# A hybrid S5/SSD/MoE block on Trainium2: the decays' bound moves from VectorE to ScalarE, and the mixers' list scheduler gets other cost estimates

## Chip, cores and metric

One core of one Trainium2 chip. The metric is the device time of one execution in microseconds (us). The kernel before takes 1853.15 us, the median of three runs.

## What is computed

One layer of a diffusion-transformer block over 256 latent tokens and 256 context tokens of width 1024, all in float32: modulation from a condition, RMS norm, one input projection, two mixers (S5, a diagonal state space with 64 groups, and SSD, a chunked scan with 32 heads in 8 groups, both in two directions), gates and an output projection, and then a mixture of 32 experts with four chosen per token.

The change touches one piece of the SSD mixer, the decay matrix of a chunk. Cut to what matters:

```
def decay_matrix(a_cum):
    mask = jnp.tril(jnp.ones((q, q), dtype=bool))
    diff = a_cum[..., :, None] - a_cum[..., None, :]
    return jnp.where(mask, jnp.exp(jnp.where(mask, diff, 0.0)), 0.0)

lmat = decay_matrix(a_cum) * dt_t[..., None, :]
y_diag = jnp.einsum('bcgls,bcgrls,bcsgrp->bclgrp', cb, lmat, x)
```

With r for the cumulated decay of the row, c for that of the column and ln dt for the logarithm of the column's step, what the kernel needs is exp(min(r - c, 0) + ln dt). The bound at 0 keeps the half outside the mask from overflowing; the mask itself comes later, with the product by `cbm`.

## The kernel before

The program has four stages. **Front**: modulation, norm and the split of the normed input into a high and a low float32r part (`uh`, `ul`). **Mixers** (`mixers`, L465 and below): the input projection and both mixers, interleaved. **Projections**: the S5 gate `glu`, the branches `wa` and `wb`, the output `wo`, the router. **Experts** (`moe`): 32 experts, each with three 1024x1024 float32 matrices, streamed as 1 MB tiles `mw`. Their loads begin in the projections, where `paced` lets out the first twelve, and not earlier.

In the mixers every piece of work is a Python generator, a stream: `gemm` (the input projection, column by column), two of `conv`, `prep`, `ssd`, `decays`, `vgen`, `tables`, `states`, `outputs`, `sigmoids` and some small ones. A stream yields before each step and names the engine that the step starts on and what it needs. `Plan.run` is a list scheduler at build time: it keeps a clock for each engine and a time at which each tile is ready, takes the stream whose next step can start first, and among those on the same engine within `NEAR` = 260 ns the one that `PRIO` and `PACE` rank first. `Planned` advances the clocks by `cost`. So the numbers in `cost` never run on the chip; they set the order in which each engine's instructions stand, and an engine runs its instructions in that order. Since all of this goes through one recording helper, the trace shows nearly every instruction of the mixers at one line (L1442), and they are told apart by tile.

The streams that matter here:

- `gemm`: for each column a weight block `w` of 128x512 is loaded, cast to `h` on ScalarE (high part), subtracted into another `h` on VectorE or GpSimd (low part; line `lo = dve if ...` picks by the planned clocks), and used in 12 matmuls into one of two PSUM banks `mm`. It prepares `LOOK` = 2 blocks ahead. Column i waits until column i-2's bank is free.
- `conv`: takes the bank of an SSD column with one ScalarE instruction and four VectorE `SCALAR_TENSOR_TENSOR` (`cv<-mm,cw,cv`); the bank is free after the fourth. A `Silu` on ScalarE follows.
- `decays`: 16 steps n (8 groups, two directions). Each loads `rt` [128, 4, 256] (one buffer), fills `et` (two buffers), turns both into exponentials, and multiplies `rt` on GpSimd. Step n+1 starts when step n has been used by `ssd`.
- `ssd`: multiplies `et` by the masked `cbm` on VectorE and runs the matmuls `yps<-et,xtok` and `yps<-rt,bt`.
- `states`, `vgen`, `outputs`: S5, mostly VectorE (`V`, `Wt`, `rot`, `Y`, `l4a`).

Before the change a decay step has eight VectorE instructions of 128x128, `et = min(rt - acs, lnd)`, with `acs` holding c - ln dt, and then one `Exp` of 128x1024 over `et` and one over `rt`.

Of the kernel before, what the change touches and what calls it, by code (L numbers as in the profile page):

```python
# [13 lines left out]
AF = mybir.ActivationFunctionType  # L14
ALU = mybir.AluOpType
# [4 lines left out]
P = 128  # L20
# [26 lines left out]
def bcast(ap, axis, n):  # L47
    a = ap.unsqueeze(axis)
    shape = list(a.shape)
    shape[axis] = n  # L50
    return a.to_broadcast(shape)


def build(tc, I, out):
    nc = tc.nc
    dve, act, pe, pool, sp = nc.vector, nc.scalar, nc.tensor, nc.gpsimd, nc.sync
# [44 lines left out]
    def aux_ps(name="aux"):  # L101
        return ps.tile([P, 512], F32, tag="aux", name=name, bufs=2)
# [221 lines left out]
    for c in range(4):  # L324
# [12 lines left out]
        for k in (2 * c, 2 * c + 1):  # L337
            h_, l_ = uh[k // 4][:, k % 4], ul[k // 4][:, k % 4]
            for wh in range(2):
                o = slice(wh * 256, wh * 256 + 256)  # L340
                a, b = sc1[:, wh, k:k + 1], modc[:, wh, 0, k:k + 1]
# [4 lines left out]
    def mm3(out, a, b, first, last):  # L346

        pe.matmul(out, a[0], b[0], start=first, stop=False)
        pe.matmul(out, a[0], b[1], start=False, stop=False)  # L349
        pe.matmul(out, a[1], b[0], start=False, stop=last)  # L350
# [24 lines left out]
    def ux(n):  # L375
        return lambda k: (uh[k // 4][:, k % 4, 0:n], ul[k // 4][:, k % 4, 0:n])
# [8 lines left out]
    def ssd_dt():  # L385
        act.activation(arow, arow, AF.Exp)
        wdh = H.tile([P, KD, 64], F32R, tag="h", name="wdh")
        act.copy(wdh, wdt)
        wdl = H.tile([P, KD, 64], F32R, tag="h", name="wdl")
        dve.tensor_tensor(wdl, wdt, wdh.bitcast(F32), op=ALU.subtract)  # L390
        pd = aux_ps()
        for k in range(KD):
            mm3(pd[0:64], (wdh[:, k], wdl[:, k]), ux(512)(k), k == 0, k == KD - 1)
        dtr = F.tile([64, 512], F32, tag="Ut", name="dtr")
        act.copy(dtr, pd[0:64])
        pt = aux_ps()
        for t in range(4):
            pe.transpose(pt[:, t * 64:(t + 1) * 64], dtr[:, t * P:(t + 1) * P], ident[0:64, 0:64])
        n = [-1]
        dtt = F.tile([P, 4, 4, 64], F32, tag="et", name="dtt", bufs=2)  # L400
        dtt = [dtt[:, i] for i in range(4)] + [F.tile([P, 4, 64], F32, tag="xtok", name="dtq", bufs=BUFS["xtok"])]

        def tt():
            n[0] += 1
            return dtt[n[0]]

        x, e, s_, s2, q = tt(), tt(), tt(), tt(), tt()
        dve.tensor_tensor(x, pt[:, 0:256].rearrange("p (t c) -> p t c", t=4), bcast(dtb, 1, 4), op=ALU.add)
        act.activation(e, x, AF.Abs)
        act.activation(e, e, AF.Exp, scale=-1.0)  # L410

        dve.tensor_scalar(s_, e, 2.0, None, op0=ALU.add)
        dve.reciprocal(s_, s_)
        dve.tensor_mul(s_, s_, e)
        dve.tensor_mul(s2, s_, s_)
        dve.tensor_scalar(q, s2, 1.0 / 15, None, op0=ALU.mult)
        for c_ in (13, 11, 9, 7, 5, 3):
            dve.scalar_tensor_tensor(q, q, 1.0 / c_, s2, op0=ALU.add, op1=ALU.mult)
        dve.scalar_tensor_tensor(q, q, 1.0, s_, op0=ALU.add, op1=ALU.mult)
        dve.tensor_scalar(x, x, 0.0, None, op0=ALU.max)  # L420
        dt = F.tile([P, 4, 64], F32, tag="dg", name="dt")
        dve.scalar_tensor_tensor(dt, q, 2.0, x, op0=ALU.mult, op1=ALU.add)
        dtA = F.tile([P, 4, 64], F32, tag="Cn", name="dtA")
        dve.scalar_tensor_tensor(dtA, dt, -1.0, bcast(arow, 1, 4), op0=ALU.mult, op1=ALU.mult)

        pr = aux_ps()
        pc = aux_ps()
        for c_ in range(2):
            for d_, tr in ((0, triU), (1, triL)):
                cols = slice(32 * d_, 32 * d_ + 32)  # L430
                pe.matmul(pr[cols, c_ * P:(c_ + 1) * P], dtA[:, c_, cols], tr, start=True, stop=True)
                pe.matmul(pc[:, c_ * 64 + 32 * d_:c_ * 64 + 32 * d_ + 32], tr, dtA[:, c_, cols], start=True, stop=True)
        arows = F.tile([64, 256], F32, tag="us", name="arows")
        act.copy(arows, pr[0:64, 0:256])
        acd = dram.tile([64, 256], F32, name="acd")
        act.dma_start(acd, arows)

        lnd = F.tile([P, 2, 64], F32, name="lnd")
        act.activation(lnd, dt[:, 0:2], AF.Ln)
        acs = F.tile([P, 2, 64], F32, name="acs")  # L440
        dve.tensor_tensor(acs, pc[:, 0:128].rearrange("p (c h) -> p c h", c=2), lnd, op=ALU.subtract)

        pw = aux_ps()
        f_, b_ = slice(0, 32), slice(32, 64)
        terms = [
            [(triLs, 2, f_), (ones, 3, f_)], [(triLs, 3, f_)],
            [(triUs, 2, b_)], [(triUs, 3, b_), (ones, 2, b_)],
            [(triLs, 0, f_)], [(triUs, 1, b_)],
            [(ones, 0, f_)], [(ones, 1, b_)],
        ]  # L450
        for i, tl in enumerate(terms):
            for j, (m_, t_, cl) in enumerate(tl):
                pe.matmul(pw[:, 32 * i:32 * i + 32], m_, dtA[:, t_, cl], start=(j == 0), stop=(j == len(tl) - 1))
        wend = F.tile([P, 8, 32], F32, name="wend")
        act.activation(wend.rearrange("p a b -> p (a b)"), pw[:, 0:256], AF.Exp)
        for i, tk, cl in ((0, 2, f_), (1, 3, f_), (2, 2, b_), (3, 3, b_), (4, 0, f_), (5, 1, b_)):
            dve.tensor_mul(wend[:, i, :], wend[:, i, :], dt[:, tk, cl])
        dsm.update(lnd=lnd, acs=acs, wend=wend, acd=acd)
# [6 lines left out]
    def mixers():  # L465
        plan = Plan(nc)
        pe, dve, act, pool, sp = plan.pe, plan.dve, plan.act, plan.pool, plan.sp
        tile_, mark, slot = plan.tile, plan.mark, plan.slot
        EP, Bb, r8, root = s5["EP"], s5["Bb"], s5["r8"], s5["root"]
        lnd, wend, acs, acd = dsm["lnd"], dsm["wend"], dsm["acs"], dsm["acd"]  # L470
# [7 lines left out]
        n = 0  # L478
# [434 lines left out]
        def decays():  # L913

            for n in range(2 * NG):
                g, d_ = n // 2, n % 2
                plan.at("decay", n / (2 * NG))
                yield ("sp", slot("rt", 1)) + ((("used", n - 1),) if n else ())
                rt = tile_(F, [P, 4, 256], F32, "rt")
                sp.dma_start(rt, acd[32 * d_ + 4 * g:32 * d_ + 4 * g + 4, :].partition_broadcast(P))  # L920
                et = tile_(F, [P, 4, 256], F32, "et", 2)
                for h in range(4):
                    yield "dve", rt
                    for c_ in range(2):
                        hh = 32 * d_ + 4 * g + h
                        dve.tensor_scalar(et[:, h, c_ * P:(c_ + 1) * P], rt[:, h, c_ * P:(c_ + 1) * P],
                                          acs[:, c_, hh:hh + 1], lnd[:, c_, hh:hh + 1], op0=ALU.subtract, op1=ALU.min)
                yield "act", et, AF.Exp
                act.activation(et, et, AF.Exp)
                act.activation(rt, rt, AF.Exp)  # L930
                yield "pool", rt, ("cv", g, 3)
                pool.tensor_tensor(rt, rt, bcast(cv[g, 3][:, 0], 1, 4), op=ALU.mult)
                dec[n] = rt, et
                mark(("dec", n))
# [332 lines left out]
    for t in range(2):  # L1267
# [15 lines left out]
                                 op0=ALU.add, op1=ALU.mult))  # L1283
# [47 lines left out]
class Plan:  # L1331
# [28 lines left out]
    def mark(self, name):  # L1360
        self.ready[name] = self.last
# [46 lines left out]
def key(x):  # L1408
    return getattr(x, "tensor", x).name


class Planned:
# [33 lines left out]
    def cost(self, op, args, kw, out, ins, n):  # L1446
        plan, name = self.plan, self.name
        if name == "pe":
            wide = ins[0]
            m = math.prod(wide.shape[1:])  # L1450
            part = 0.25 if m <= 32 else 0.5 if m <= 64 else 1
            if op == "transpose":
                return 109 * wide.shape[0] / P
            return max(n, 16) * (4 if ins[1].dtype == F32 else 1) * 0.42 * part
        if name == "act":
            f = next((a for a in args if isinstance(a, AF)), None)
            table = plan.SETS.get(f, plan.table)
            switch, plan.table = 1280 * (table != plan.table), table
            return 60 + 0.85 * n + switch
        if name == "pool":  # L1460
            return 80 + 2.2 * n
        if op == "tensor_tensor_scan":
            return 63 + 2.1 * n
        if op == "reciprocal":
            return 63 + 6.3 * n
        fast = op in ("tensor_copy", "tensor_scalar") and not any(key(a) in plan.psum for a in (out, *ins))
        return 63 + (0.52 if fast else 1.05) * n


class Shared:  # L1470
# [476 lines left out]
```

## Time and profile before

| what | value |
|---|---|
| median of three runs | 1853.15 us (1849.97 to 1854.26) |
| profiled execution, its own time | 1846.35 us |
| its span | 1844.2 us |
| TensorE matmul busy | 1589.1 us, 86% |
| VectorE busy | 904.5 us, 49% |
| ScalarE busy | 506.8 us, 27% |
| GpSimd busy | 290.0 us, 16% |
| granted TensorE clock, mean | 0.934 |
| HBM read | 529.60 MB |

Busy shares are means over the four stages, which have different limits, so each stage is read by itself. "X <- Y" in the table of waits means that X's engine sat idle until Y finished. Granted clock is a share of full speed: 1.0 is 2.4 GHz and 0.5 is 1.2 GHz. DMA is the mean busy share of 16 engines.

### The profile page before, as it was taken

The numbers are of one execution on the slowest core, as the hardware profiler recorded it, in microseconds if no ns is written. First come the engines' busy times: TensorE is split into PE (matmuls) and PEld (weight loads), VectorE is DVE, ScalarE is ACT, GpSimd is POOL, SyncE is SP. The second block draws the span as 40 slices with busy tenths as digits, with TensorE's granted clock in tenths as the row PEclk, the third lists the DMA queues.
The fourth block names the chain that finished last, engine by engine and source line by source line (L and its number), as shares of the span: only waits on it lengthen the run. The fifth ranks groups of instructions, "written<-read, shape, count | busy, mean of one in ns | idle before, by whom it ended". The sixth has DMA issues, their size and how long they took to land. (4 is left out here: it accounts for less than half of the span.)

```text
span 1844.2 us, 27968 instructions
## 1 busy us (share of the span) xinstructions
PE 1589.1 (86%) x11118; PEld 935.1 (51%) x11118; DVE 904.5 (49%) x1671; ACT 506.8 (27%) x893; POOL 290.0 (16%) x297
## 2 busy tenths in 40 slices
PE   6798888976988799897998888898888889988987
PEld 3576666764766698783533232333333444333443
DVE  7668899888898546664222222242222223212233
ACT  5333453552435565342111111111111111111111
POOL 5133445435331330100000000000000000000000
PEclk8899898987997999998999999999999999988998
DMA  8677554444542357784999999999998999999984
GB/s 309 181 236 237 178 144 136 119 121 110 148 127 64 114 155 264 235 281 161 417 418 417 417 418 417 413 418 417 418 410 350 418 417 418 418 417 419 418 349 174
DMA packets 141415, 539.36 MB, mean 292 GB/s; under 512 B 31736, under 2 KB 44952, under 8 KB 91920
## 3 DMA queue, kind: packets, MB, share of 16 engines
q1 hardware_dynamic: 136032, 526.95, 75.7%
q10 hardware_dynamic: 4608, 7.95, 1.3%
q8 instruction: 143, 2.34, 0.5%
q0 software_dynamic: 560, 1.52, 0.3%
q14 instruction: 72, 0.59, 0.1%
HBM read 529.60 MB, written 6.77 MB: 291 GB/s over the span
## 5 line engine op out<-in xcount | busy, mean ns | idle before, releaser
L1519 PE MATMUL p_gu<-mw,xe 128*64 128x512 f32 x2048 | 474.8, 601 | 45.2 <-DMA mw<-in_mu 28.4
L1442 PE MATMUL mm<-uh,h 128*128 128x256 f32 (+1 forms) x1152 | 323.6, 361 | 45.2 <-DVE cv L1442 29.9
L1519 PEld LDWEIGHTS p_gu<-mw,xe 128*64 128x64 f32 x2048 | 174.2, 137 | 335.7 <-issue 176.8
L1442 PEld LDWEIGHTS mm<-uh,h 128*128 128x128 f32 x1152 | 209.6, 201 | 85.4 <-issue 42.3
L1629 PE MATMUL p_y<-mw,aT 128*64 128x512 f32 x1024 | 243.4, 627 | 3.4 <-issue 3.4
L1442 PE MATMUL mm<-ul,h 128*128 128x256 f32 (+1 forms) x576 | 202.5, 352 | 0.0
L1442 POOL TENSOR_TENSOR h<-w,h 128x512 fp32r<-128x512 f32 x99 | 150.3, 1522 | 279.3 <-ACT h L1442 213.6
L1637 DVE SCALAR_TENSOR_TENSOR yw<-p_y,gs,xq 64x512 f32<-64x512 f32 x64 | 48.0, 750 | 287.3 <-PE p_y L1629 286.2
L1629 PEld LDWEIGHTS p_y<-mw,aT 128*64 128x64 f32 x1024 | 75.3, 144 | 147.4 <-issue 144.0
L1442 ACT CAST h<-w 128x512 fp32r<-128x512 f32 x144 | 88.1, 618 | 168.7 <-PE mm L1442 121.2
L1442 PEld LDWEIGHTS mm<-ul,h 128*128 128x128 f32 x576 | 116.0, 201 | 13.5 <-issue 3.1
L1533 DVE TENSOR_SCALAR au<-p_gu 128x512 f32<-128x512 f32 x32 | 22.1, 692 | 198.7 <-PE p_gu L1519 198.7
L1639 ACT CAST yh<-yw 64x512 fp32r<-64x512 f32 x64 | 39.4, 616 | 285.4 <-DVE yw L1637 285.4
L1527 DVE TENSOR_SCALAR ag<-p_gu 128x512 f32<-128x512 f32 (+1 forms) x34 | 23.0, 676 | 169.8 <-PE p_gu L1519 169.8
L1442 DVE SCALAR_TENSOR_TENSOR cv<-mm,cw,cv 128x508 f32<-128x508 f32 (+3 forms) x128 | 85.6, 673 | 11.0 <-ACT cv L1442 10.6
L359 DVE TENSOR_TENSOR low<-w,hi 128x512 fp32r<-128x512 f32 x80 | 59.6, 751 | 41.6 <-ACT hi L357 40.3
L1528 ACT ACTIVATE as<-ag 128x512 f32<-128x512 f32 (+1 forms) x34 | 21.0, 617 | 210.5 <-DVE ag L1527 210.5
L1442 ACT ACT_TABLE_LOAD x55 | 70.6, 1283 | 29.9 <-DVE cv L1442 29.1
L357 ACT CAST hi<-w 128x512 fp32r<-128x512 f32 x80 | 49.4, 620 | 70.3 <-PE mm L349 24.8
L1613 PE MATMUL p_t<-ident,au 128*128 128x128 f32 x128 | 30.5, 325 | 39.7 <-PEq L1730 25.2
L1442 DVE TENSOR_SCALAR et<-rt,acs,lnd 128x128 f32<-128x128 f32 x128 | 45.9, 413 | 23.6 <-DMA rt<-acd 23.4
L1442 DVE TENSOR_TENSOR h<-w,h 128x512 fp32r<-128x512 f32 x45 | 39.2, 872 | 31.8 <-ACT h L1442 31.8
(452 smaller groups left out, 2335.2 us busy)
## 6 DMA issues: line engine op xcount, KB each, us to landing
mw<-in_mg SPq DMA_DIRECT2D x128, 1024.0 KB
mw<-in_mu SPq DMA_DIRECT2D x128, 1024.0 KB
mw<-in_md SPq DMA_DIRECT2D x128, 1024.0 KB
w<-in_wg SPq DMA_DIRECT2D x96, 256.0 KB
ada<-in_ada SPq DMA_DIRECT2D x32, 256.0 KB
Toe<-in_ada SPq DMA_DIRECT2D x16, 512.0 KB
vT<-Ed SPq DMA_DIRECT2D x16, 512.0 KB
l8a<-in_ada SPq DMA_DIRECT2D x16, 512.0 KB
```

The source lines that it names most:

```text
L357: act.copy(hi, w)
L359: lo.tensor_tensor(low, w, hi.bitcast(F32), op=ALU.subtract)
L1442: return fn(*args, **kw)
L1519: mm = pe.matmul(dst[c * q:c * q + c, 0:n], lhs(k), w[:, o:o + n], start=(i == 2 and k == 0), stop=(k == KD - 1))
L1527: dve.tensor_scalar(g_, pg, 7.0, None, op0=ALU.min)
L1528: sg = act.activation(s_, g_, AF.Sigmoid, scale=1.702)
L1533: dve.tensor_scalar(u_, pu, -7.0, 7.0, op0=ALU.max, op1=ALU.min)
L1613: pe.transpose(pa[:, q * P:(q + 1) * P], u_[:, q * P:(q + 1) * P], ident)
L1629: self.done = pe.matmul(py[64 * q:64 * q + 64], aT[:, k % 4, k // 4], wts[e, 2, c // load.unit][:, c % load.unit:c % load.unit + 512], sta ...
L1637: dve.scalar_tensor_tensor(w[rows], self.py[rows], self.gs[rows, nh, j:j + 1], gf[rows, 512 * nh:512 * nh + 512], op0=ALU.mult, op1=ALU.mult)
L1639: act.copy(self.hi[rows, nh], w[rows])
```

## The change

```
-        dve.tensor_tensor(acs, pc[:, 0:128].rearrange("p (c h) -> p c h", c=2), lnd, op=ALU.subtract)
+        dve.tensor_copy(acs, pc[:, 0:128].rearrange("p (c h) -> p c h", c=2))
...
-                for h in range(4):
-                    yield "dve", rt
-                    for c_ in range(2):
-                        hh = 32 * d_ + 4 * g + h
-                        dve.tensor_scalar(et[:, h, c_ * P:(c_ + 1) * P], rt[:, h, c_ * P:(c_ + 1) * P],
-                                          acs[:, c_, hh:hh + 1], lnd[:, c_, hh:hh + 1], op0=ALU.subtract, op1=ALU.min)
+                for f, src, by in ((AF.Relu, rt, acs), (AF.Exp, et, lnd)):
+                    for h in range(4):
+                        yield "act", src, f
+                        for c_ in range(2):
+                            hh = 32 * d_ + 4 * g + h
+                            cl = slice(c_ * P, c_ * P + P)
+                            act.activation(et[:, h, cl], src[:, h, cl], f, scale=-1.0, bias=by[:, c_, hh:hh + 1])
                 yield "act", et, AF.Exp
-                act.activation(et, et, AF.Exp)
                 act.activation(rt, rt, AF.Exp)
...
-            return 60 + 0.85 * n + switch
+            return (330 if hasattr(kw.get("scale"), "shape") else 150) + 0.89 * n + switch
         if name == "pool":
-            return 80 + 2.2 * n
+            return 300 + 2.3 * n
         if op == "tensor_tensor_scan":
-            return 63 + 2.1 * n
+            return 115 + 2.1 * n
         if op == "reciprocal":
-            return 63 + 6.3 * n
-        fast = op in ("tensor_copy", "tensor_scalar") and not any(key(a) in plan.psum for a in (out, *ins))
-        return 63 + (0.52 if fast else 1.05) * n
+            return 145 + 6.3 * n
+        if op == "tensor_scalar":
+            return 280 + 0.48 * n
+        if op == "scalar_tensor_tensor":
+            return 200 + 1.06 * n
+
+        shared = not any(key(a) in plan.psum for a in (out, *ins))
+        return (145 + 1.04 * n) * (1.2 if shared else 1)
```

A decay step now has eight `Relu` of 128x128 on ScalarE, relu(c - r), and eight `Exp` of 128x128, exp(ln dt - relu(c - r)), each with a pointer to one column as its bias; `rt`'s own `Exp` stays. `acs` holds c alone. The new estimates change the planned order of nearly everything in the mixers, and with it two counts: of the 144 low parts `h`, VectorE now has 53 and GpSimd 91 (45 and 99 before), and ScalarE loads a table 49 times (55 before). Everything else has the same number of instructions on the same engine.

VectorE, where the first decay step stood, before:

```order
L1442 SCALAR_TENSOR_TENSOR Wt<-Wt,vtw 128x512
L1442 TENSOR_TENSOR vtw<-EP,Ct 128x512
L1442 TENSOR_TENSOR h<-w,h 128x512
L1442 TENSOR_SCALAR et<-rt,acs,lnd 128x128 x8
L1442 TENSOR_TENSOR h<-w,h 128x512
L1442 SCALAR_TENSOR_TENSOR cv_1002<-mm,cw,cv_1002 128x2x254
```

and now:

```order
L1442 SCALAR_TENSOR_TENSOR Wt<-Wt,vtw 128x512
L1442 TENSOR_TENSOR h<-w,h 128x512
L1442 TENSOR_TENSOR vtw<-EP,Ct 128x512
L1442 TENSOR_TENSOR h<-w,h 128x512
L1442 SCALAR_TENSOR_TENSOR cv_990<-mm,cw,cv_990 128x2x254
L1442 SCALAR_TENSOR_TENSOR cv_990<-mm,cw,cv_990 128x2x255
L1442 TENSOR_TENSOR h<-w,h 128x512
```

The eight bounds are gone from ahead of the first column's conv; the low parts stand nearer to each other.

ScalarE at one of the first decay steps, before:

```order
L1442 ACT_TABLE_LOAD
L1442 ACTIVATE et<-et 128x1024
L1442 ACTIVATE rt<-rt 128x1024
L1442 CAST h<-w 128x512 x2
```

and now, at the third:

```order
L1442 ACTIVATE et<-rt,acs 128x128 x8
L1442 ACTIVATE cv_1892<-cv_1892 128x512
L1442 CAST h<-w 128x512
L1442 ACT_TABLE_LOAD
L1442 ACTIVATE et<-et,lnd 128x128 x8
L1442 ACTIVATE rt<-rt 128x1024
L1442 ACTIVATE cv_2072<-mm,cbias,cw 128x512
L1442 CAST h<-w 128x512 x2
```

Two instructions became seventeen, and the casts `h` of the gemm stand behind them. Of the 16 `Relu` groups 13 stand unbroken like this; of the `Exp` groups 6.

VectorE behind the third of the four pairs of scans `Y<-R,Y`, its last rows up to the end of the next conv, before (14 rows stand between the scans and this conv's first instruction):

```order
L1442 TENSOR_TENSOR h<-w,h 128x512
L1442 TENSOR_TENSOR rot<-Y,T 128x256 x2
L1442 SCALAR_TENSOR_TENSOR cv_4599<-mm,cw,cv_4599 128x2x254
L1442 TENSOR_TENSOR l4a<-rot 64x128 x4
L1442 SCALAR_TENSOR_TENSOR cv_4599<-mm,cw,cv_4599 128x2x255
L1442 TENSOR_TENSOR V<-V,vT 128x4x128
L1442 SCALAR_TENSOR_TENSOR cv_4599<-mm,cw,cv_4599 128x2x255
L1442 TENSOR_TENSOR V<-V,vT 128x4x128
L1442 SCALAR_TENSOR_TENSOR cv_4599<-mm,cw,cv_4599 128x2x254
```

and now:

```order
L1442 TENSOR_TENSOR et<-et,xl 128x4x128
L1442 SCALAR_TENSOR_TENSOR cv_5154<-mm,cw,cv_5154 128x2x254
L1442 SCALAR_TENSOR_TENSOR cv_5156<-mm,cw,cv_5156 128x2x254
L1442 SCALAR_TENSOR_TENSOR cv_5154<-mm,cw,cv_5154 128x2x255
L1442 SCALAR_TENSOR_TENSOR cv_5156<-mm,cw,cv_5156 128x2x255
L1442 SCALAR_TENSOR_TENSOR cv_5154<-mm,cw,cv_5154 128x2x255
L1442 SCALAR_TENSOR_TENSOR cv_5156<-mm,cw,cv_5156 128x2x255
L1442 SCALAR_TENSOR_TENSOR cv_5154<-mm,cw,cv_5154 128x2x254
L1442 SCALAR_TENSOR_TENSOR cv_5156<-mm,cw,cv_5156 128x2x254
```

The convs of two columns now take turns, so both banks `mm` come free together; 19 rows stand between the scans and the first of them.

## Rows read from the trace of the kernel before

**Rows 1.** Busy time by stretch (us, matmul, weight load, VectorE, ScalarE, GpSimd, clock, DMA share, GB/s).

```profile
49.00:684.00 635.00, 535.16 (x4906) 426.32 (x4905) 504.87 (x943) 281.94 (x460) 246.82 (x229) 0.90 0.51 148
180.00:333.00 153.00, 127.63 (x1175) 100.30 (x1177) 138.18 (x263) 65.78 (x105) 77.07 (x97) 0.88 0.50 143
395.00:570.00 175.00, 136.23 (x1116) 105.49 (x1118) 152.79 (x288) 67.10 (x108) 71.64 (x68) 0.86 0.40 115
684.00:850.00 166.00, 140.54 (x1069) 132.12 (x1068) 111.59 (x213) 77.43 (x148) 14.09 (x7) 0.93 0.71 239
880.00:1760.00 880.00, 787.25 (x4363) 320.69 (x4363) 220.16 (x346) 101.70 (x196) 0.00 (x0) 0.97 1.00 413
```

**Rows 2.** Expert loads: count, duration, first and last start in us.

```profile
L1856 SPq DMA_DIRECT2D mw<-in_mg x128: 327/328/2254, 689.5 to 1776.8; - x128
```

**Rows 3.** TensorE's waits in the mixers, 49 to 684 us (total, times, longest).

```profile
PE mm L1442 <- DVE cv L1442: 29.9, 8, 11.8
PE yps L1442 <- DVE et L1442: 15.5, 8, 6.2
PE mm L1442 <- POOL h L1442: 9.0, 3, 4.3
PE aux L1442 <- DVE dg L1442: 6.6, 4, 4.1
PE s L1442 <- DVE V L1442: 4.4, 5, 1.6
PE aux L1442 <- DVE xw L1442: 4.3, 1, 4.3
PE mm L1442 <- DVE h L1442: 3.6, 2, 3.3
PE y L1442 <- DVE l4a L1442: 3.4, 2, 2.0
PE aux L1442 <- ACT zt L1442: 2.3, 1, 2.3
PE s L1442 <- ACT vtv L1442: 2.1, 2, 1.9
```

**Rows 4.** The longest of these waits, in the timeline: scans on VectorE, then TensorE.

```profile
419.57 4.46 DVE L1442 TENSOR_TENSOR_SCAN Y<-R,Y 128x1024 f32<-128x1024 f32 x2
...
441.99 0.77 PE L1442 MATMUL mm<-uh,h 128*128 128x512 f32 x1 [11.85 <-DVE cv L1442]
```

**Rows 5.** Groups of instructions that the change removes or moves (busy us, mean ns).

```profile
L1442 DVE TENSOR_SCALAR et<-rt,acs,lnd 128x128 f32<-128x128 f32 x128 | 45.9, 413 | 23.6 <-DMA rt<-acd 23.4
L1442 DVE TENSOR_TENSOR h<-w,h 128x512 fp32r<-128x512 f32 x45 | 39.2, 872 | 31.8 <-ACT h L1442 31.8
L1442 ACT ACTIVATE et<-et 128x1024 f32<-128x1024 f32 x16 | 17.0, 1060 | 21.4 <-DVE et L1442 21.3
L1442 ACT ACT_TABLE_LOAD x55 | 70.6, 1283 | 29.9 <-DVE cv L1442 29.1
```

**Rows 6.** ScalarE instructions near the new ones: small, with and without a pointer bias.

```profile
L1442 ACT COPY strip<-w 128x128 f32<-128x128 f32 x16 | 4.2, 265 | 7.0 <-PE w L1442 6.9
L439 ACT ACTIVATE lnd<-dt 128x128 f32<-128x128 f32 x1 | 0.3, 310 | 0.0
L210 ACT ACTIVATE s5small<-s5small,halfpi 128x64 f32<-128x64 f32 x1 | 0.3, 348 | 0.0
L342 ACT ACTIVATE uh<-xT,modc,sc 128x256 fp32r<-128x256 f32 x16 | 8.2, 591 | 6.7 <-DVE sc L336 6.7
L209 ACT ACTIVATE s5small<-s5small 128x64 f32<-128x64 f32 x1 | 0.2, 239 | 0.0
```

**Rows 7.** Timelines: four of them in a row on ScalarE; three gemm matmuls on TensorE.

```profile
44.02 2.08 ACT L342 ACTIVATE uh<-xT,modc,sc 128x256 fp32r<-128x256 f32 x4 [2.35 <-DVE sc L336]
...
426.25 0.63 PE L1442 MATMUL mm<-uh,h 128*128 128x512 f32 x2
426.72 0.40 PE L1442 MATMUL mm<-ul,h 128*128 128x512 f32 x1
426.95 0.63 PE L1442 MATMUL mm<-uh,h 128*128 128x512 f32 x2
```

## Prediction

> **What bounds the kernel now.** I read the stretches first, because the four stages have different limits [rows 1]. From 880 us on the DMA share is 1.00 at 413 GB/s: the experts' matrices set the pace there, and no engine does. That stage has a fixed length, and what can move is its start. The first expert load goes out at 689.5 us [rows 2], just behind the mixers, which end at 684 us; `paced` lets none out earlier. So whatever the mixers win or lose moves everything behind them by as much, and the change touches the mixers alone.
>
> In the mixers (49 to 684 us) DMA is at 0.51, GpSimd at 247 and ScalarE at 282 of 635 us. TensorE is busy 535.2 us, so it idles 99.8 us; VectorE is busy 504.9 us. The stage ends on TensorE, with the last gate columns, so TensorE's waits are what counts. They are read next [rows 3]: the seven rows in which it waits for VectorE add up to 67.7 us (29.9 + 15.5 + 6.6 + 4.4 + 4.3 + 3.6 + 3.4), the longest for GpSimd to 9.0, and the two longest for ScalarE to 4.4. Two stretches hold most of it: from 180 to 333 and from 395 to 570 us VectorE is busy 138.2 of 153 and 152.8 of 175 us, and TensorE idles there 25.4 + 38.8 = 64 of its 100 us, at a granted clock of 0.88 and 0.86 [rows 1]. The longest wait shows the mechanism [rows 4]: VectorE's scans begin at 419.57, the conv that frees a bank stands behind them and other S5 work, and TensorE stands still 11.85 us, until 441.99. VectorE's queue is the bound of the mixers.
>
> **The change, part by part.** *VectorE.* The 128 bounds go: 45.9 us busy [rows 5]. Eight more low parts come, 8 x 0.872 = 7.0 us [rows 5]. Net 38.9 us less, of 504.9. `acs` becomes a copy of the same size: nothing, it is one instruction. Where VectorE is the bound a microsecond of it is a microsecond of the end; where it is not, TensorE's own work covers it. The two stretches above hold 138.2 + 152.8 = 291.0 of its 504.9 us, 58%. So 0.58 x 38.9 = 22.4 us come off the path. The bounds: nothing, if the order puts the convs no earlier, and 67.7 us, if all waits for VectorE go.
>
> *The wait for `rt`.* VectorE idled 23.4 us ahead of the bounds until `rt` had landed [rows 5], with everything behind it in its queue held up. This wait moves to ScalarE. By the same 58% that is 13.6 us at most; I take half, 6.8, since in the stretches where VectorE is late the load has mostly landed (bounds 0 and 13.6).
>
> *The clock.* A mean of 0.88 and 0.86 between the levels 1.0 (2.4 GHz) and 0.5 (1.2 GHz) means 24% of 153 us and 28% of 175 us at the lower one, 86 us together, and the low stretches are those with the waits [rows 1]. At the lower level TensorE does half, so up to 43 us are lost there. Of its 100 us of idle time 29 would go, so 0.29 x 43 = 12.5 us at most come back; where VectorE sets the pace a faster TensorE wins nothing, and I take half, 6 (bounds 0 and 12.5).
>
> *ScalarE.* No row has the new instruction, 128x128 out of SBUF with a pointer as bias. From below: the 128x128 copy without one, 265 ns [rows 6]. From above: 310 ns for 128x128 without a pointer, and the step from 239 to 348 ns that a pointer makes at 128x64, 109 ns: 419 ns [rows 6]. In a run they overlap: four of 591 ns each took 2.08 us [rows 6, 7], so (4 x 591 - 2080) / 3 = 95 ns each. I take 419 - 95 = 324 ns, because the new ones stand in runs of eight. 256 x 0.324 = 83 us come (68 to 107); the 16 long exponentials go, 17.0 us, and six table loads, 6 x 1.283 = 7.7 us [rows 5]. Net +58 us (43 to 83): ScalarE goes from 44% to some 56% of the stage. What hides this is the gemm's look-ahead of two blocks. Three matmuls take 0.70 us at full clock [rows 7], so a block of twelve 512-wide ones takes 2.8 us and a 256-wide one 1.4 us; two blocks cover 5.6 or 2.8 us. An unbroken `Relu` run is 0.42 + 7 x 0.324 = 2.7 us: covered. A table load, an `Exp` run and `rt`'s own `Exp` are 1.28 + 2.7 + 1.06 = 5.0 us: covered behind wide columns, 2.2 us too long behind narrow ones. Six `Exp` groups stand unbroken; half of 6 x 2.2 us is 6.6, and I take +6 (0 to the first rival's price).
>
> The Trainium skill ("ScalarE: Activation LUTs", What ACT_TABLE_LOAD costs) gives such an instruction 280 ns + 0.833 ns per element and an overlap of about 93 ns back to back. By that the 256 would come to an estimated 75 us; the trace's overlap of 95 ns agrees.
>
> *GpSimd* loses eight low parts; it is waited for little [rows 3], and I count nothing.
>
> **The sum.** -22.4 - 6.8 - 6 + 6 = -29 us, from the profiled execution's 1846.35 us to some 1817 us. The median of the runs shown stands 6.8 us above it, so the forecast is 1853.15 - 29 = **1824 us**. Its own range is 1800 to 1845 us: -53 with the upper bounds of the `rt` and clock terms and half as much again in the VectorE term, -8 with half of the VectorE term and 16 us for ScalarE.
>
> **Rivals.** *ScalarE becomes the feeder (slower).* Its queue is in order, and the gemm's casts `h` stand behind the decays. If runs do not overlap, a `Relu` run is 8 x 0.419 = 3.35 us and an `Exp` run with its table load and `rt` 5.7 us; behind narrow columns they are 0.55 and 2.9 us too long, and 16 steps of 3.45 us are 55 us of TensorE waiting. Against the 35 us of the other terms that is +20 us: 1873 us. It decides from 35/16 = 2.2 us per step on. For it: the wait for `rt` now stands ahead of casts as well, and the planner counts 264 ns (150 + 0.89 x 128) where I count 324. Against it: ScalarE idles 353 of 635 us now, and TensorE hardly waits for it [rows 1, 3]. The Trainium skill ("ScalarE: Activation LUTs", Rules for kernel authors) speaks for this rival: relu and min belong on VectorE, not on ScalarE. By that rule the time would be this rival's; the trace does not bear it out for this stage, where VectorE is the busier one. Chance 0.17.
>
> *The new order gives it back.* The estimates reorder all queues, and behind the third pair of scans the new order lets two convs take turns, so both banks come free together and behind 19 rows: the wait of 11.85 us would stay there [rows 4]. If three such waits come anew, 36 us, the 35 us are gone: 1853 us. For it: this one place. Against it: it is less work on the engine that is late, in any order. Chance 0.17.
>
> *All waits for VectorE go*, 67.7 us [rows 3]: 1785 us. For it: the old estimates put a 128x512 VectorE instruction at 63 + 1.05 x 512 = 601 ns where the row has 872 [rows 5], so the planned order was made for a faster VectorE than there is; the new ones give (145 + 1.04 x 512) x 1.2 = 813 ns. Against it: VectorE still has 466 us of work in the stage. Chance 0.13.
>
> **The numbers.** Forecast 0.53, and 0.17, 0.17 and 0.13 as above. A change of under 0.2%, 3.7 us, is about what a measurement of this kernel cannot tell from none. Faster by more: 0.53 + 0.13 and 0.05 of the second rival, 0.71; within: 0.08 of the second; slower: its last 0.04 and the first, 0.21. The range that leaves out half of the third rival and somewhat over half of the first is 1794 to 1860 us.
>
> **What would show it.** Right: the mixers end near 655 us instead of 684 and the first expert load goes out some 29 us earlier; the stretch behind it keeps its length at DMA 1.00; TensorE's waits for `cv` and `et` shrink, its idle time in the mixers falls from 100 to some 75 us, and its clock rises above 0.90; the new ScalarE instructions stand at 0.4 us alone, and runs of eight at 2.7 us. Wrong: TensorE or GpSimd waits for `h` from ScalarE by tens of microseconds (first rival), or waits for `cv` of 10 us and more stand behind the scans as before (second). If the mixers end earlier and the total does not, my reading of the experts' stage is wrong.

## The result, and the profile after

The change is slower: 1862.63 us against 1851.17 us, medians of 20 runs each on one chip, a ratio of 1.0057 [1.004, 1.0074]. I had forecast 1824 us. The profiled execution of the changed kernel takes 1865.1 us (span 1863.1).

The tile view of `mm` tells where the mixers end: at the last start of the group `mm<-uh,h`. Before:

```profile
L1442 PE MATMUL mm<-uh,h x1152: 276/387/988, 49.6 to 684.3; 128*128 128x256 f32 x106, 128*128 128x512 f32 x86
```

After, with the expert loads under it:

```profile
L1442 PE MATMUL mm<-uh,h x1152: 274/392/797, 48.9 to 698.6; 128*128 128x256 f32 x106, 128*128 128x512 f32 x86
```

```profile
L1861 SPq DMA_DIRECT2D mw<-in_mg x128: 327/328/446, 703.8 to 1795.9; - x128
```

The mixers end 14.3 us later, and the first expert load goes out 14.3 us later (689.5 before, [rows 2]). The loads then take 1092.1 us instead of 1087.3, at 411 instead of 413 GB/s. In the kernel before and those below that have the full work this stretch lies between 1087.3 and 1099.4 us (`e15`), so those 4.8 us are not told from scatter. So the question is why the mixers became longer, and the last gemm matmul is the measure used below: it is free of what the expert loads do from run to run. It is one profiled execution each time, though. The medians of the totals are a check on it: here they are 11.5 us apart, where the mixers' ends are 14.3, and for the kernels below the two differ by up to 9 us. A few microseconds in the mixers' end alone show nothing.

Windows of the changed kernel (us, matmul, weight load, VectorE, ScalarE, GpSimd, clock, DMA share, GB/s), the mixers as a whole first:

```profile
49.00:698.60 649.60, 539.39 (x4906) 433.91 (x4905) 471.10 (x822) 331.53 (x695) 237.80 (x223) 0.89 0.50 145
180.00:333.00 153.00, 129.79 (x1179) 104.60 (x1169) 122.47 (x206) 83.28 (x170) 70.03 (x66) 0.92 0.55 158
395.00:570.00 175.00, 133.58 (x1159) 107.01 (x1159) 129.17 (x229) 89.62 (x184) 65.48 (x63) 0.84 0.41 117
480.00:638.00 158.00, 121.28 (x1086) 97.57 (x1089) 133.23 (x233) 80.56 (x165) 56.20 (x59) 0.78 0.32 91
880.00:1760.00 880.00, 785.16 (x4191) 310.50 (x4188) 220.24 (x342) 101.59 (x194) 0.00 (x0) 0.97 1.00 411
```

The stretch that lost most, before:

```profile
480.00:638.00 158.00, 131.88 (x1254) 103.69 (x1252) 129.56 (x241) 74.89 (x112) 54.28 (x31) 0.90 0.37 108
```

VectorE did lose its work: 471.1 us in the mixers, where 504.9 stood [rows 1]. In the two stretches in which I took it for the bound it is now busy 122 of 153 and 129 of 175 us (138 and 153 before). TensorE got nothing for it. It idles 649.6 - 539.4 = 110.2 us in the mixers (99.8 before), at a clock of 0.89 (0.90). From 480 to 638 us it is busy 10.6 us less than before and does 1086 matmuls instead of 1254, at a clock of 0.78 instead of 0.90.

TensorE's waits in the mixers after the change (total, times, longest), to be held against [rows 3]:

```profile
PE yps L1442 <- DVE et L1442: 21.9, 10, 5.7
PE mm L1442 <- DVE cv L1442: 20.1, 10, 5.8
PE y L1442 <- DVE l4a L1442: 13.9, 4, 9.0
PE mm L1442 <- POOL h L1442: 6.5, 3, 4.9
PE aux L1442 <- DVE xw L1442: 4.7, 2, 3.1
PE aux L1442 <- ACT cv L1442: 4.4, 4, 2.8
PE s L1442 <- ACT vtv L1442: 3.4, 2, 1.9
```

The wait for `cv` shrank from 29.9 to 20.1 us, and those for `et` and `l4a` grew from 15.5 to 21.9 and from 3.4 to 13.9. The sum of the first three was 48.8 and is 55.9. Summed over all rows of this view, the waits for VectorE are 74.6 us (73.2 before), though it has less to do, and those for ScalarE 17.4 (8.6 before). The place that I had pointed at, behind the third pair of scans, shows it in the timeline (start, duration, what; the bracket is the idle time before and its releaser):

```profile
475.18 4.47 DVE L1442 TENSOR_TENSOR_SCAN Y<-R,Y 128x1024 f32<-128x1024 f32 x2
...
482.48 0.64 PE L1442 MATMUL y<-Wt,l4a 128*32 128x128 f32 x2 [8.98 <-DVE l4a L1442]
...
490.02 0.63 PE L1442 MATMUL y<-Wt,l4a 128*32 128x128 f32 x2 [2.66 <-DVE l4a L1442]
...
494.73 5.32 DVE L1442 SCALAR_TENSOR_TENSOR cv<-mm,cw,cv 128x508 f32<-128x508 f32 x8
...
499.45 0.79 PE L1442 MATMUL mm<-uh,h 128*128 128x512 f32 x1 [3.74 <-DVE cv L1442]
```

Both columns' convs stand in one piece at 494.73, 15 us behind the end of the scans. Neither bank is free until then: no gemm matmul runs between the one at 469.40 and the one at 499.45, and TensorE does the `y` matmuls piece by piece as VectorE delivers `l4a`.

The new ScalarE instructions themselves cost about what I had said (groups: busy us, mean ns, idle time ahead):

```profile
L1442 ACT ACT_TABLE_LOAD x49 | 62.9, 1283 | 26.0 <-DVE cv L1442 16.8 <-DVE et L1442 8.4
L1442 ACT ACTIVATE et<-et,lnd 128x128 f32<-128x128 f32 x128 | 41.6, 392 | 0.2
L1442 ACT ACTIVATE et<-rt,acs 128x128 f32<-128x128 f32 x128 | 40.0, 390 | 20.7 <-DMA rt<-acd 20.7
```

81.6 us for the 256 (83 predicted), and a run of eight takes 2.45 us in the timeline (2.7 predicted).

### The profile page after: what moved, and what is told of

Same layout as the page of the kernel before. It is cut to its first block, busy times and chain, and to the rows that moved or that the text cites. A ratio compares the mean times of both kernels' runs of the same rounds, so it can differ in the third digit from the quotient of the medians.

```text
span 1863.1 us, 28046 instructions
## 1 busy us (share of the span) xinstructions
PE 1589.5 (85%) x11118; PEld 936.8 (50%) x11118; DVE 870.0 (47%) x1551; ACT 556.2 (30%) x1127; POOL 280.1 (15%) x289
## 5 line engine op out<-in xcount | busy, mean ns | idle before, releaser
L1442 PE MATMUL mm<-uh,h 128*128 128x256 f32 (+1 forms) x1152 | 326.5, 364 | 34.2 <-DVE cv L1442 20.1
L1524 PEld LDWEIGHTS p_gu<-mw,xe 128*64 128x64 f32 x2048 | 169.6, 137 | 346.3 <-issue 170.4
L1442 PEld LDWEIGHTS mm<-uh,h 128*128 128x128 f32 x1152 | 215.0, 206 | 72.7 <-issue 23.7
L1442 POOL TENSOR_TENSOR h<-w,h 128x512 fp32r<-128x512 f32 x91 | 141.5, 1559 | 320.4 <-ACT h L1442 249.2
L1442 DVE SCALAR_TENSOR_TENSOR cv<-mm,cw,cv 128x510 f32<-128x510 f32 (+3 forms) x128 | 84.1, 672 | 17.3 <-ACT cv L1442 16.5
L1442 ACT ACT_TABLE_LOAD x49 | 62.9, 1283 | 26.0 <-DVE cv L1442 16.8
L1618 PE MATMUL p_t<-ident,au 128*128 128x128 f32 x128 | 29.9, 319 | 36.7 <-PEq L1735 22.5
L1619 ACT COPY aT<-p_t 128x256 f32<-128x256 f32 x64 | 23.8, 372 | 108.1 <-PE p_t L1618 108.0
```

The costliest lines, as they stand in the source:

```text
L1442: return fn(*args, **kw)
L1524: mm = pe.matmul(dst[c * q:c * q + c, 0:n], lhs(k), w[:, o:o + n], start=(i == 2 and k == 0), stop=(k == KD - 1))
L1618: pe.transpose(pa[:, q * P:(q + 1) * P], u_[:, q * P:(q + 1) * P], ident)
L1619: act.copy(aT[:, 2 * h:2 * h + 2].rearrange("p a b s -> p (a b s)"), pa[:, 256 * h:256 * h + 256])
```

## Experiments

Two theories stood at the start. **Work**: moving the decays costs more on ScalarE than it saves on VectorE. **Order**: the new estimates, and any change of the work, give another order of the queues, and what an order is worth outweighs the work in it. Most kernels below use a small hook: the planner plans one list of instructions, and at issue others are put in the places of some of them (`plan.instead`). So the order of one kernel can carry the work of another.

### The two halves of the change, and the two orders

`e1` is the change without the new estimates, `e2` the new estimates alone. `e3` is planned like the kernel before, instruction for instruction, and issues the change's work in the same places:

```
+  plan.instead = lambda: nc.scalar.activation(et.., rt.., AF.Relu, scale=-1.0, bias=acs..)
   dve.tensor_scalar(et.., rt.., acs.., lnd.., op0=ALU.subtract, op1=ALU.min)
...
+  plan.instead = exps      # eight Exp of 128x128
   act.activation(et, et, AF.Exp)
```

`e4` is the reverse: planned like the change, bounds issued on VectorE and one long `Exp` on ScalarE.

> The decays on ScalarE, the planner's old estimates. Theory O (the new order loses more than the moved work wins): faster than before by 10 to 30 us, since VectorE has 46 us less to do. Theory S (ScalarE feeds the gemm late): slower than before by 5 to 20 us, about as the change itself.

> The new estimates, the decays still bounded on VectorE. Theory O: slower than before by 20 to 40 us. Theory S: no slower than before, within 5 us of it or faster.

> Planned as before, instruction by instruction, but where the plan puts a bound on VectorE the program issues the Relu on ScalarE, and where it puts the long exponential the program issues the eight short ones: the moved work in the old order. Theory O: faster than before by 15 to 30 us. Theory S: slower than before by 5 to 20 us.

> Planned as the changed kernel, but each planned Relu is issued as a bound on VectorE and the eight planned Exp as one long exponential at the place of the last: the new order without the moved work. Theory O: slower than the changed kernel by 10 to 30 us. Theory S: faster than the changed kernel by 5 to 20 us.

Each ratio is to the kernel before as measured beside it (1852.5 us for `e1` to `e4`, 1851.17 for the change).

| kernel | order of | work of | last gemm matmul | median | ratio to before |
|---|---|---|---|---|---|
| before | before | before | 684.3 | 1852.5 | |
| e3 | before | change | 688.0 | 1856.41 | 1.0028 [1.0004, 1.0052] |
| e4 | change | before | 711.3 | 1873.68 | 1.0129 [1.0102, 1.0156] |
| change | change | change | 698.6 | 1862.63 | 1.0057 [1.004, 1.0074] |
| e1 | old estimates, planned anew | change | 696.8 | 1864.14 | 1.0078 [1.0057, 1.0099] |
| e2 | new estimates | before | 739.3 | 1898.25 | 1.0253 [1.023, 1.0275] |

The two rows that complete the square, `e3` and then `e4`:

```profile
L1454 PE MATMUL mm<-uh,h x1152: 274/389/988, 51.7 to 688.0; 128*128 128x256 f32 x106, 128*128 128x512 f32 x86
```

```profile
L1449 PE MATMUL mm<-uh,h x1152: 276/390/796, 52.0 to 711.3; 128*128 128x256 f32 x106, 128*128 128x512 f32 x86
```

The four in the square say it: in the old order the move costs 3.7 us of the mixers, in the new order it saves 12.7. The new order costs 27.0 us with the old work and 10.6 with the new. By the medians of the totals these four are +3.9, -9.7, +21.2 and +7.6 us. The order is the larger term, and it has cost what the move could have won. Neither theory as I had put it foretold all four kernels: by the order alone `e1` and `e3` should have been faster than before, by the work alone `e2` no slower than before and `e4` faster than the change, and none of that came true.

The loss does not need the new estimates: `e1`, planned with the old ones, ends where the change does. They make no better orders by themselves either: `e2` ends latest of all these. TensorE's waits there for `rt` from GpSimd make 19.7 us, second only to those for `cv`, and made 0.8 us before; why the more exact numbers plan worse stays open.

### What the bounds on VectorE cost: nothing, or 27 us

`e5` keeps the order of before and leaves the bounds out; `e7` keeps it and issues each bound twice; `e8` keeps it and issues them on GpSimd.

```
e5:  plan.instead = lambda: 1                                   # no bound
     plan.instead = lambda: nc.scalar.activation(et, rt, AF.Exp, scale=0.0)
e7:  nc.vector.tensor_scalar(et.., rt.., acs.., lnd.., ...)     # once more, unplanned
e8:  plan.instead = lambda: nc.gpsimd.tensor_scalar(et.., rt.., acs.., lnd.., ...)
```

> Planned as before, but the 128 bounds are left out: et is the exponential of 0 and not of the decay, so the experts may be chosen otherwise and only the end of the mixers is to be compared. VectorE has 46 us less to do and ScalarE no more than before. Theory C (relief and load cancel): the last gemm matmul starts 20 to 35 us before 684 us. Theory L (the mixers wait in loops over several engines, and no engine's sum of work sets their end): within 8 us of 684.

> Planned as before, and each of the 128 bounds is issued twice on VectorE: 46 us more there. Theory V (VectorE sets the end, and what held it when the bounds were left out was something that came just behind it): slower than before by 25 to 50 us. Theory G (the bounds stand where VectorE would wait anyway): within 10 us of before.

> Planned as before, the bounds issued on GpSimd in place of VectorE, the long exponential stays. VectorE has 46 us less, ScalarE no more. Theory G: no faster than before, since VectorE's relief wins nothing; slower by up to 20 us where low parts stand behind the bounds on GpSimd. Theory V: faster by 10 us or more.

Without any bound, and nothing in their place, the mixers end where they ended (`e5`):

```profile
L1445 PE MATMUL mm<-uh,h x1152: 274/388/988, 50.6 to 684.1; 128*128 128x256 f32 x106, 128*128 128x512 f32 x86
```

With each bound twice (`e7`):

```profile
L1444 PE MATMUL mm<-uh,h x1152: 274/391/797, 50.5 to 711.3; 128*128 128x256 f32 x106, 128*128 128x512 f32 x86
```

So 46 us more on VectorE cost 27.0 us (28.9 by the medians), and 46 us less win 0.2; the 20 to 35 us that I had expected if the relief was worth something did not come. (`e5`'s total of 1875.57 us is no measure: it leaves out the decays, and its expert loads take 1117.1 us.) The timeline of `e5` at the longest wait shows why, next to [rows 4]:

```profile
409.12 0.94 DVE L1445 TENSOR_TENSOR vtv<-V,vT 128x512 f32<-128x512 f32 x1 [3.23 <-DMA V<-Bd]
...
421.25 5.51 DVE L1445 TENSOR_TENSOR_SCAN Y<-R,Y 128x1024 f32<-128x1024 f32 x2
...
443.67 0.77 PE L1445 MATMUL mm<-uh,h 128*128 128x512 f32 x1 [12.25 <-DVE cv L1445]
```

and the same place before:

```profile
407.38 0.48 DVE L1442 SCALAR_TENSOR_TENSOR ybT<-mb,ssdn,aux 128x256 f32<-128x256 f32 x1 [1.90 <-PE aux L1442]
```

Before, VectorE is busy without a gap of over 0.3 us from 407.38 us, where it had waited for TensorE, to the conv that ends the wait at 441.99. No bound stands in that stretch. Taking bounds out earlier only made VectorE wait longer at its start (there 3.23 us for a transfer), and the wait of 11.85 us became one of 12.25. I followed all of TensorE's waits of 1 us or more for VectorE back in this way, through the timeline of before, to VectorE's last gap of over 0.3 us. They are 18 and make 62.0 us. Ten of them, 36.2 us, have no bound in the unbroken stretch that leads to them; the other eight could give back some 17 us at most, if each shortens by the bounds ahead of it. In `e5` 19 such waits make 57.1 us, up to 444 us mostly at the same places. What went there came back elsewhere: summed over all rows of the waits, those for VectorE fell from 73.2 to 65.6 us, while those for GpSimd grew from 9.8 to 15.2 and those for transfers from 8.4 to 11.6.

`e8` ends the mixers at 740.6 us and takes 1908.92 us, 1.0315 [1.0289, 1.034]. On GpSimd a bound takes 905 ns where VectorE took 413 [rows 5]:

```profile
L926 POOL TENSOR_SCALAR et<-rt,acs,lnd 128x128 f32<-128x128 f32 x128 | 114.1, 905 | 28.9 <-DMA rt<-acd 27.6 <-DVE h L1445 1.3
```

```profile
ACT h L1445 <- PE mm L1445: 113.9, 52, 10.9
ACT et L1445 <- POOL et L926: 96.4, 16, 11.1
```

ScalarE waits 96.4 us for them, with the casts `h` queued behind, and TensorE's waits for ScalarE make 49.6 us, where 8.6 stood: the mechanism of my first rival, on another engine and at a price that decides. I had expected 20 us of loss at most.

### What the decays on ScalarE cost

`e6` keeps order and bounds of before, issues 128 spare `Relu` on top and 128 short `Exp` in place of the 16 long ones. `e11` plans anew, with eight `Relu` on ScalarE and the long `Exp` kept; it leaves out the factor dt, so only its mixers are compared. `e12` replaces the eight bounds by one minimum and brings c and ln dt in by the bias of eight short `Exp`, so the total work is smaller than in either kernel:

```
+  dve.tensor_tensor(et.., rt.., bcast(acs..), op=ALU.min)       # 128x1024, one per step
+  act.activation(et[:, h, cl], et[:, h, cl], AF.Exp, bias=lnd..)   # lnd holds ln dt - c
```

> Planned as before, the bounds stay on VectorE, and ScalarE does the new work on top: 128 Relu into a spare tile and 128 short exponentials in place of 16 long ones. Theory C: slower than before by 20 to 35 us. Theory L: within 8 us of before.

> Old estimates; the Relu goes to ScalarE, but one long exponential without bias follows, so the factor dt is left out of et (only the mixers' end is compared). Half of the new load, all of the relief. If the cost goes by the load: the mixers end at 670 to 682 us. If any work on ScalarE ahead of the exponential costs all of it: 690 to 700 us.

> Old estimates, correct output: one VectorE instruction of 128x1024 takes min(r, c) for a whole step, and eight short exponentials on ScalarE add ln dt - c as their bias. VectorE is relieved of some 25 us, ScalarE gets some 23 us. At the rates of the runs so far (27 us won for 46, 40 lost for 66): within 10 us of before.

`e6` ends the mixers at 699.6 us and takes 1.0118 [1.009, 1.0146]: an addition to ScalarE alone, 11 more table loads among it, costs 15.3 us in this execution, the shortest of its six, and 19.7 by the medians. In the same order the exchange (`e3`, also 66 table loads) ends at 688.0 and the bounds' absence (`e5`, 61) at 684.1, so with VectorE relieved the decays on ScalarE cost 3.9. `e11` ends at 694.2 us, and not at the 670 to 682 that half of the load would have given; `e12` ends at 701.8 (1862.1 us, 1.005 [1.003, 1.007]), within the 10 us of before that I had expected. Both were planned anew, both have less work than the change, and neither reaches 684: they do not separate the work from the order.

### What an order is worth

If the order weighs so much, a change without any meaning must move the time as much. `p1` sets the planner's window for choosing by priority, `NEAR`, from 260 to 240 ns. `p2` and `p4` count every cost but the transfers' 2% higher, in the kernel before and in the change. `e9` plans and runs without the bounds, `e13` is `e9` with costs 2% higher, and `e10` is `e9` with 256 ScalarE instructions added that nobody waits for:

```
p1:        -NEAR = 260                                 +NEAR = 240
p2,p4,e13: -cost = self.cost(op, args, kw, out, ins, n)
           +cost = 1.02 * self.cost(op, args, kw, out, ins, n)
e9:        -dve.tensor_scalar(et.., rt.., acs.., lnd.., ...)   (all eight)
           -act.activation(et, et, AF.Exp)      +act.activation(et, rt, AF.Exp, scale=0.0)
e10:       +act.activation(spare, lnd.., f, scale=-1.0, bias=acs..)   (Relu, then Exp)
```

> The kernel before with NEAR = 240 for 260: same work, another order. Theory T (the order before is one that suits its constants, and nearly any other costs): slower than before by 8 to 40 us. Otherwise: within 4 us.

> The kernel before with every planned cost, DMA apart, times 1.02: same work, estimates no better and no worse, another order. Theory T: slower than before by 8 to 40 us. Otherwise: within 4 us.

> The changed kernel with every planned cost, DMA apart, times 1.02: the same work in another order. Theory T (the constants suit one order and a new order costs 5 to 40 us by chance): some 5 to 15 us to either side of the changed kernel, at or above the time before. If the measured estimates make orders worse by themselves: slower than the changed kernel by 10 us or more.

> As the run with the bounds left out (et is the exponential of 0, so only the mixers' end is compared), but the planner knows it and orders anew with its old estimates. If only the fixed order held the relief back: the last gemm matmul starts 15 to 35 us before 684 us. If the relief is worth nothing in any order: 680 us or later, give or take what any new order costs.

> The bounds left out and planned so, with every planned cost times 1.02 (et is the exponential of 0; only the mixers' end is compared). If the 27 us are the relief: the last gemm matmul starts at 650 to 672 us. If they are one lucky order: at 675 us or later.

> The bounds left out and planned so, as in the run that ended its mixers at 657 us, but with 256 ScalarE instructions of 128x128 in the stream of the decays behind each step, out of a constant tile into a spare one, so that nothing waits for them (et is the exponential of 0; only the mixers' end is compared). If ScalarE's load costs: the last gemm matmul starts at 685 to 700 us. If the longer chain of the decays costs: at 655 to 670 us.

`e9` and then `e13`:

```profile
L1436 PE MATMUL mm<-uh,h x1152: 274/386/988, 49.1 to 657.2; 128*128 128x256 f32 x106, 128*128 128x512 f32 x86
```

```profile
L1436 PE MATMUL mm<-uh,h x1152: 276/391/796, 51.3 to 697.7; 128*128 128x256 f32 x106, 128*128 128x512 f32 x86
```

By itself `e9` would have made the theory of work: leave the bounds out, plan anew, win 27.1 us. `e13` has the same work, and 2% on all costs takes 40.5 us away. The totals of the kernels that leave out the decays can be held against each other, and agree: `e9` takes 1848.93 us, `e5` 1875.57 and `e13` 1887.98. `p1` ends at 688.0 us (1.0025 [1.0009, 1.004]), `p2` at 697.6 (1.0071 [1.0043, 1.0099]), `p4` at 702.2 (1.0068 [1.0046, 1.009]). If nearly any new order costs, `p1` and `p2` should have lost 8 to 40 us each: `p2` did, `p1` did not. `p4` stayed within 4 us of the change. `e10` ends at 667.8, 10.6 us behind `e9` for 103 us of added ScalarE time and 18 more table loads, but in an order of its own.

The last two test whether `e9`'s order is a good one for real work. Both are planned like `e9`; `e14` issues the change's sixteen instructions on ScalarE in the place of each long `Exp`, `e15` the eight bounds on VectorE ahead of it:

```
   yield "act", rt, AF.Exp
+  plan.instead = decay       # e14: 8 Relu, 8 Exp;  e15: 8 bounds on VectorE, then the long Exp
   act.activation(et, rt, AF.Exp, scale=0.0)
```

> The order is the one that the scheduler planned for mixers without the bounds (whose last gemm matmul stood at 657.2 us), and the full work is issued in it, the decays on ScalarE as in the change: eight Relu and eight exponentials in the place of each long exponential. Nothing is left out. Theory (the order decides, by tens of microseconds, and the work put into a good order pays a part of its own time): the added ScalarE time is that of the addition to the old order, 699.6 - 684.3 = 15.3 us, or less, so the last gemm matmul stands at 660 to 675 and the whole takes 1828 to 1845 us, 7 to 24 below the kernel before. Rival (a good order is good only for the durations that it was planned with): the mixers lose what a replanning loses, the last gemm matmul stands at 684 or later and the whole at 1852 or more.

> The same planned order as in the run beside it, with the bounds issued on VectorE at the place of each long exponential and the exponential kept long, so the work is that of the kernel before. Theory (the order decides): VectorE's added 46 us cost here what the second 46 us cost in the old order, 711.3 - 684.1 = 27, so the last gemm matmul stands near 684 and the whole near 1852; on ScalarE (the run beside it) it is at least 8 us earlier. Rival (the place of the work is nothing, only the order counts): both runs end within 4 us of each other.

`e14`, then `e15`:

```profile
L1448 PE MATMUL mm<-uh,h x1152: 275/390/988, 49.7 to 693.9; 128*128 128x256 f32 x106, 128*128 128x512 f32 x86
```

```profile
L1447 PE MATMUL mm<-uh,h x1152: 275/385/796, 47.9 to 679.5; 128*128 128x256 f32 x106, 128*128 128x512 f32 x86
```

The order lost its lead as soon as work was put into it: by these executions 22.3 us with the bounds on VectorE (27 was my estimate) and 36.7 with the decays on ScalarE (15.3 was). My expectation for `e14` failed, and the numbers of its rival came true, the mixers' end beyond 684 and the total beyond 1852 us. Its reason, that an order is good only for the work that it was planned for, did not: `e15` borrows its order and ends its mixers 4.8 us earlier than the kernel before, the only kernel with the full work that does.

How far apart `e14` and `e15` are stays open. The mixers' ends say 14.4 us, but `e14`'s profiled execution is the longest of its twelve, 13 us above their median. The medians say 3.4: `e14` takes 1854.01 us, 1.0013 [0.9992, 1.0034], and `e15` 1850.66, 0.9994 [0.9976, 1.0013], neither told from before. By them the rival of `e15`, that only the order counts and the place of the work is nothing, stands as well. No version beat the kernel before.

All orders together, by the last gemm matmul, with the median against the kernel before as measured beside it:

| work | last gemm matmul in these orders | mean | median against before, in the same sequence | mean |
|---|---|---|---|---|
| of the kernel before | 679.5 (e15), 684.3 (before), 688.0 (p1), 697.6 (p2), 711.3 (e4), 739.3 (e2) | 700.0 | -1.1, 0, 3.9, 13.3, 21.2, 45.8 | 13.8 |
| of the change | 688.0 (e3), 693.9 (e14), 696.8 (e1), 698.6 (change), 702.2 (p4) | 695.9 | 3.9, 2.3, 11.6, 11.5, 12.6 | 8.4 |

(The number of low parts on VectorE, 44 to 53, and of table loads differs a little within a row of the table.) Over the orders the two works are 4 us apart (5 by the medians), while the orders of one work spread over 60 us and over 14; with so few orders that is no difference. In the three orders that were run with both works the move is worth +3.7, -12.7 and +14.4 us by the mixers' ends, +3.9, -9.7 and +3.4 by the medians. The kernel before has the second best of its six orders. A change that makes the planner draw again has to win some 16 us (700.0 - 684.3) before it breaks even; that is an estimate from six orders, and 8 us of it come from `e2` alone.

One thing speaks against a mere draw. The three orders that were planned for the change's work (`e1`, the change, `p4`) end within 5.4 us of each other, and both borrowed ones (`e3`, `e14`) end before them. Whether that is chance, or the planner serves this work badly, no run here settles.

## Why the prediction was wrong, point by point

- **What bounds the kernel.** Right: the experts' stretch kept its length within 0.5%, and what the mixers lost moved its start by as much.
- **"Where VectorE is the bound a microsecond of it is a microsecond of the end", -22.4 us.** This step failed. VectorE's busy time in the mixers fell by 33.8 us (38.9 predicted), but in the old order the absence of the bounds, with the wait for `rt` off VectorE's queue, won 0.2 us (`e5`). I took a busy share of 87 to 90% in a stretch for a bound. Of the waits that count the larger part began behind points at which VectorE itself had waited, for another engine or a transfer, and no bound stands between those points and the wait. The trace of before would have told: 36.2 of 62.0 us of waits have no bound in the stretch that leads to them. Nor is it a constant of the work. In the change's own order the whole exchange wins 12.7 us, and in the order of `e15` leaving the bounds out (`e9`) wins 22.3 (one execution each). The step holds for added work (27.0 us for 46, `e7`), which is not its mirror image.
- **The wait for `rt`, -6.8 us.** Nothing came of it: ScalarE now idles 20.7 us for `rt`, and `e5`, where VectorE no longer waits for it either, contains its worth.
- **The clock, -6 us.** It did not come: TensorE idles 110.2 us instead of the 75 predicted, and the clock is 0.89 instead of above 0.90.
- **ScalarE, +6 us.** Right in size for the old order, +3.9 (`e3` against `e5`), and the duration of the instruction was right. But it is no constant: +15.3 as an addition (`e6`), and in `e9`'s order 14.4 us more than the bounds by the mixers' ends and 3.4 by the medians. The rule of the Trainium skill that I had weighed ("ScalarE: Activation LUTs", Rules for kernel authors: min and relu belong on VectorE) agrees with the old order by 3.7 us and goes against the runs in the change's order, by 12.7; in `e9`'s order the medians do not tell.
- **First rival, ScalarE as feeder.** Not what happened: none of TensorE's seven longest waits after the change is for an `h` from ScalarE, and its waits for `h` make 2.5 us. Its waits for ScalarE did double, to 17.4 us, but with the old work in the same order (`e4`) they are 16.8, so that is the order too.
- **Second rival, "the new order gives it back".** It is what happened, and more: the result is 11.5 us behind the kernel before and not level with it. I gave it 0.17 and put it at nothing in the sum. I had seen the place, and priced it as a few waits that stay; the sign that I named, waits for `cv` of 10 us and more, did not show (the longest is 5.8), since the time there went into waits for `l4a`. I left out that the new order changes every wait in 635 us. Measured, the order alone is +10.6 us with the new work and +27.0 with the old. Along the old order the result is -0.2 (no bounds) + 3.9 (decays on ScalarE) + 10.6 (the new order) = 14.3 us, where my sum had -29. My argument against it, "less work on the engine that is late, in any order", fell with the VectorE step.
- **Third rival**, 1785 us: the waits for VectorE stayed at 55.9 us in the three longest rows alone.
- **The range** of 1794 to 1860 us ended 2.6 us below the result. Had the order been counted as a term of its own, from nothing to some tens of microseconds, it would have held it.

## What to carry to other kernels

Ask of each removed instruction not whether its engine is busy, but whether it stands between the wait that you want to shorten and the last point at which that engine itself waited; only there does it shorten the wait directly. Adding work to a static order cost 27.0 us here, while removing as much from the same order won nothing, so an experiment that adds does not price a removal. And where a list scheduler sets the order, try meaningless changes first (2% on all costs): their spread is the bar that a change has to clear. Here 2% moved the mixers' end of the change by 3.6 us, of the kernel before by 13.3 and of the kernel without bounds by 40.5, and the change's own 14.3 us lie within that. To tell work from order, issue the work of one plan in the order of the other.

## What the runs showed of the hardware

- The same VectorE bound took 371 ns on average in one order (`e2`) and 451 in another (`p2`), 413 before; `h` of 128x512 took 743 (`e11`) to 916 ns (`e6`). Behind the mean of 413 stand these durations in the kernel before (least, middle and greatest, ns):

```profile
L1442 DVE TENSOR_SCALAR et<-rt,acs,lnd x128: 319/341/1453, 84.9 to 638.6; 128x128 f32<-128x128 f32 x128
```

Sorted by GpSimd's records in the same trace, the 97 bounds that overlap no GpSimd instruction took 319 to 349 ns, and the 31 that do took 641 ns on average. GpSimd's own `h` took 1394 (`p4`) to 1638 ns (`e2`), while the 128x128 ScalarE instruction with a pointer stayed at 390 to 402 ns on average in every run that has it. The Trainium skill ("SBUF — State Buffer", Who interferes with whom) says that of the engines only VectorE and GpSimd share a port; these durations agree with it, though no run here took GpSimd's work away.

- A 128x128 bound with two pointers takes 905 ns on GpSimd against 413 on VectorE, 2.2 times as long.
- Executions of one kernel differ by over 1% (1844 to 1867 us for `e14`), so totals of single runs could not have told these kernels apart. The end of the mixers in one execution is not free of this: in seven of the fourteen other kernels with the full work, what it says against the kernel before and what the medians of the totals say are 3.7 to 9.3 us apart.
